# A hybrid decoder layer on one core: full-array recurrence products, paired value products, a new order of the output projection, and new costs in the kernel's planning clock

## The chip, the cores and the metric

One of the eight cores of a Trainium2 chip runs the whole layer in one launch. The metric is device time in microseconds (us), from the first to the last instruction and what little lies around them. TensorE (PE) multiplies, VectorE (DVE), ScalarE (ACT) and GpSimd (POOL) work on vectors, and SyncE (SP) issues the DMAs. The program is static: each engine works through its own list in order, and a step waits by semaphores for steps of other engines.

## The reference

512 tokens of width 2048. A combined projection of the normed input feeds three branches; their gated outputs are concatenated, projected again and added to x.

```python
h = _rms(x, norm_g[l]); proj = h @ w_in[l]
pa, pb, pc = _split(proj, (A_COLS, B_COLS, C_COLS))
ya = _rwkv7(...) * silu(ga)            # 12 heads of 64; recurrence below
yb = _pool(pu, ...) * silu(pg)         # trailing means, 4 groups
yc = _stick_breaking(qc, kc, vc, ...) * silu(gc)   # 12 heads of 64, strictly causal
x = x + concatenate([ya, yb, yc]) @ w_out[l]

def step(state, inp):                  # per token, 64x64 state per head
    sa = einsum('bhvk,bhk->bhv', state, -kk_t)
    state = state * w_t + sa x (kk_t * a_t) + v_t x k_t
    return state, einsum('bhvk,bhk->bhv', state, r_t)
```

## The kernel before

**Projections.** The input projection has 57 column tiles of 128. Each tile is the sum over 16 slices of D of three products (`three`: high by high, high by low, low by high part), that is 48 matmuls of 128x128 by 128x512 into a PSUM tile `pj`; the first three tiles (`first`) are made while the inputs arrive, so 54 tiles or 2592 matmuls are `pj`. The output projection has 4 column groups `nb`; each is 192 such matmuls (tile `oacc`), 768 in all, which go over 8 pairs of slices of the branch outputs (`i2`). Before group 0 uses a slice, `split_y` splits it into `yh` (ACT) and `yl` (DVE). Every 128x1024 piece of weights is fetched by SP (`raw`) and split by ACT (`wh`) and DVE (`wl`).

**Branch steps.** The heads go in six pairs. The generators `rwkv(p)`, `attention(p)` and `pooling(g)` issue the branch work between the projection's matmuls: after each of them `pump()` lets every generator go on whose time has come. That time comes from `Pace`, a clock that the kernel keeps while it is built: it adds an assumed cost to `now` for each matmul and to a due time for each result, and `need(..., margin=)` says from when a step may be issued. `pump(True)` issues whatever is next without asking for the time. A list scheduler behind the kernel orders each engine's list, guided by program order and its own costs.

**One pair of the recurrence.** `rwkv(p)` makes decays and keys (`dec`, `av`, `ss`: products of 512 columns), then `bk` and `amr`, whose products `gm` give the triangular blocks `lt` and `rx`. The blocks of `lt` go to DRAM (`s1`), come back as `nblk` and `xblk`, are inverted in 30 steps on DVE (`pr`, `xblk`), go back through `s2` into `lt` and are completed by two groups of 32x32 products (`q1`, `q2`). Then 8 chunks of 64 tokens follow one another, each a chain: product `w`, copy to `wsb`, product `u`, copies into `uv`, product `s`, new state `uv` of the next chunk. The output `y` has two more products. Each of the five products is one of 64 columns per head, in its half of the array's rows or columns. At the end come norm sums (`bn`, `mu`, `var`) and the gate. Pair p+1 starts its `amr` when pair p's chunks are issued. Attention has score products `z` (the low part over half the rows), scans on DVE, transposes `wT`, and value products `o` per head.

**The end.** Before the output projection the kernel drains all generators by `pump(True)`; the pooling products wait for the last pair. The order of the slices is a0 to a5, c0 to c5, b0 to b3.

Of the kernel before, what the change touches and what calls it, by code (L numbers as in the profile page):

```python
# [8 lines left out]
F32 = mybir.dt.float32  # L9
# [43 lines left out]
BANKS = {"pj": 2, "g": 3, "c": 3}  # L53
# [150 lines left out]
def hybrid_trunk_kernel(ctx: ExitStack, tc: tile.TileContext, x, xT, w_in, w_out, vecs, consts, up_w, pool_w, out, tap=None):  # L204
# [15 lines left out]
    tp = ctx.enter_context(tc.tile_pool(name="tp", bufs=14))  # L220
# [57 lines left out]

    hh = [hp.tile([P, T], F32R, tag=f"hh{k}", name=f"hh{k}") for k in range(KT)]
# [14 lines left out]
    for pl, tag, parts in ((ap, "q2", 1), (ap, "k2", 1), (ap, "w3", 1), (rp, "bk", 2), (rp, "bkt", 2), (rp, "rx", 2),  # L294
                           (rp, "uv", 2), (rp, "amr", 3), (ap, "wt", 2)):
        xt = pl.tile([P, parts, T], F32, tag=tag, name=name("x"))
# [209 lines left out]
    def rwkv(p):  # L506
# [13 lines left out]
        mm(dec, upl[lo, 0:P], wd2[lo, :], False, True)  # L520
# [4 lines left out]
        mm(av, upl[hi, P:2 * P], ad2[hi, :], False, True)  # L525
# [35 lines left out]
        amr = rp.tile([P, NC_, 3, C], F32, tag="amr", name=name("amr"))  # L561
        for h, s in ((0, lo), (1, hi)):
# [7 lines left out]
        dve.tensor_tensor(amr[:, :, 2, :], r3, e[:, :, 1:], ALU.mult)  # L570
# [7 lines left out]
        lt = rp.tile([P, NC_, C], F32, tag="lt", name=name("lt"))  # L578
        ms = strict.rearrange("p (o t) -> p o t", o=1)
        mi = incl.rearrange("p (o t) -> p o t", o=1)  # L580
        for half in range(2):
            cs = slice(4 * half, 4 * half + 4)
            for h, s, other in quad:
                yield need(*([amr, bk] if half == 0 and h == 0 else []), tag="g")
# [6 lines left out]
                dve.tensor_tensor(lt[s, cs, :], g4[s, :, 0, :], ms[s].to_broadcast([HD, 4, C]), ALU.mult)  # L591
# [6 lines left out]
        for h in range(2):  # L598
            for b in range(2):
                r0 = h * HD + b * B  # L600
                dma(out=s1v[:, :, h, b, :], in_=lt[r0:r0 + B, :, b * B:(b + 1) * B])
# [30 lines left out]
        for h in range(2):  # L632
            for b in range(2):
                r0 = h * HD + b * B
                dma(out=lt[r0:r0 + B, :, b * B:(b + 1) * B], in_=s2v[:, :, h, b, :])
# [416 lines left out]
```

## Time and profile before

| | |
|---|---|
| median of 3 runs | 1089.75 us (1088.41 to 1089.97) |
| the profiled execution | 1089.68 us, span 1088.0 us |
| PE busy | 1066.2 us (98%) |
| DVE, ACT, POOL busy | 737.6 (68%), 427.8 (39%), 143.1 us (13%) |

The profile counts PE as busy while a matmul is anywhere in its pipeline, so a share of 98% says that it seldom stood empty, not that it worked at its peak. What a step costs is read from the start of the last matmul before it to the start of one behind it.

### The profile page before, as it was taken

To read this page: it belongs to the slowest core of one execution; us is meant where nothing else is said; L and a number is where in the kernel's file an instruction comes from. 1 tells how busy PE (TensorE), PEld (TensorE's weight loads), DVE (VectorE), ACT (ScalarE), POOL (GpSimd) and SP (SyncE) were. 2 spreads that over 40 slices of the span, in tenths; PEclk is the share of its full clock that TensorE was granted. 3 is DMA by queue.
4 is the path that set the end of the run, shared out by engine and by line. 5 is a ranking of instruction groups with operands and counts; after the bars stand their busy time and mean duration, and the time that the engine had idled before them with its cause. 6 is when DMAs were issued, how large, how long until landed. Compare 5 with 4: busy or idle time off the path is not lost.

```text
span 1088.0 us, 14731 instructions
## 1 busy us (share of the span) xinstructions
PE 1066.2 (98%) x5552; PEld 801.3 (74%) x5552; DVE 737.6 (68%) x1596; ACT 427.8 (39%) x670; POOL 143.1 (13%) x208
## 2 busy tenths in 40 slices
PE   9998999999999999999999999999999999999998
PEld 7877766687666877668766787667776677888887
DVE  6266978759787797778877799777986457223232
ACT  6453525235353354334543345524443235111111
POOL 0031113101132011210211102210021111000000
PEclk9999999999999999899999999999999999999999
DMA  9513231132211321113221132112221125444232
GB/s 329 204 63 105 80 93 40 56 92 84 84 48 51 107 85 66 58 59 97 86 76 39 64 115 77 61 58 84 100 78 55 48 94 163 149 154 137 96 137 75
DMA packets 58185, 101.92 MB, mean 94 GB/s; under 512 B 29312, under 2 KB 30720, under 8 KB 58112
## 3 DMA queue, kind: packets, MB, share of 16 engines
q1 hardware_dynamic: 58112, 100.96, 28.2%
q8 instruction: 44, 0.72, 0.3%
q14 instruction: 29, 0.24, 0.1%
HBM read 95.17 MB, written 5.77 MB: 93 GB/s over the span
## 4 chain that ended last, share of the span: by engine, by line
PE 80%; DVE 10%; issue 4%; ACT 2%; DMA 2%; POOL 2%; SPq 0%; POOLq 0%; DVEq 0%; ACTq 0%
PE pj L350 45%; PE oacc L350 15%; PE first L350 3%; PE o L350 2%; PE z L350 2%; DVE w L198 2%; DVE wl L198 2%; PE gm L350 2%; PE y L350 2%; PE w L350 2%; PE wT L354 1%; DVE xblk L198 1%; PE u L350 1%; POOL e L198 1%; PE s L350 1%
## 5 line engine op out<-in xcount | busy, mean ns | idle before, releaser
L350 PE MATMUL pj<-hl,wh 128*128 128x512 f32 x864 | 349.0, 404 | 0.0
L350 PE MATMUL pj<-hh,wh 128*128 128x512 f32 x864 | 347.9, 403 | 1.0 <-DVE u L198 0.8
L350 PE MATMUL pj<-hh,wl 128*128 128x512 f32 x864 | 347.6, 402 | 0.0
L198 DVE TENSOR_TENSOR wl<-raw,wh 128x1024 fp32r<-128x1024 f32 x140 | 172.1, 1229 | 168.6 <-ACT wh L198 162.8
L198 ACT CAST wh<-raw 128x1024 fp32r<-128x1024 f32 x140 | 147.0, 1050 | 312.7 <-PE pj L350 187.5
L350 PEld LDWEIGHTS pj<-hh,wh 128*128 128x128 f32 x864 | 163.1, 189 | 38.0 <-issue 4.4
L350 PEld LDWEIGHTS pj<-hh,wl 128*128 128x128 f32 x864 | 163.2, 189 | 35.4 <-issue 0.4
L350 PEld LDWEIGHTS pj<-hl,wh 128*128 128x128 f32 x864 | 163.1, 189 | 35.5 <-issue 1.2
L350 PE MATMUL oacc<-wl,yh 128*128 128x512 f32 x256 | 100.1, 391 | 0.8 <-DVE wl L198 0.8
L350 PE MATMUL oacc<-wh,yl 128*128 128x512 f32 x256 | 99.6, 389 | 0.0
L350 PE MATMUL oacc<-wh,yh 128*128 128x512 f32 x256 | 99.6, 389 | 0.0
L198 POOL TENSOR_SCALAR e<-e 128x512 f32<-128x512 f32 x28 | 49.0, 1749 | 327.9 <-ACT e L198 327.6
L198 POOL TENSOR_TENSOR d<-u 128x512 f32<-128x512 f32 x25 | 34.2, 1370 | 230.9 <-DVE u L198 148.6
L350 PEld LDWEIGHTS oacc<-wl,yh 128*128 128x128 f32 x256 | 48.0, 188 | 11.5 <-DVE wl L198 1.3
L350 PEld LDWEIGHTS oacc<-wh,yl 128*128 128x128 f32 x256 | 48.1, 188 | 10.0 <-issue 0.2
L350 PEld LDWEIGHTS oacc<-wh,yh 128*128 128x128 f32 x256 | 48.0, 188 | 10.0
L198 DVE TENSOR_TENSOR xblk<-xblk,pr 128x60 f32<-128x60 f32 (+8 forms) x180 | 44.5, 247 | 4.1
L198 ACT ACTIVATE e<-e 128x512 f32<-128x512 f32 x50 | 31.4, 629 | 39.1 <-POOL e L198 38.8
L198 DVE TENSOR_TENSOR_SCAN w<-kon,n 128x512 f32<-128x512 f32 (+3 forms) x48 | 39.3, 841 | 6.6 <-POOL n L198 6.5
L198 DVE TENSOR_TENSOR pr<-xblk,nblk 128x60 f32<-128x60 f32 (+8 forms) x180 | 38.7, 215 | 4.4
L198 DVE TENSOR_TENSOR u<-pj,rstd 128x512 f32<-128x512 f32 x50 | 34.3, 686 | 8.3 <-PE pj L350 7.9
L198 ACT ACTIVATE n<-n 128x512 f32<-128x512 f32 (+1 forms) x72 | 38.9, 557 | 1.3
(195 smaller groups left out, 1262.7 us busy)
## 6 DMA issues: line engine op xcount, KB each, us to landing
raw<-in_w_in SPq DMA_DIRECT2D x108, 512.0 KB, 3.4
raw<-in_w_out SPq DMA_DIRECT2D x32, 512.0 KB, 3.4
xs<-in_x SPq DMA_DIRECT2D x8, 512.0 KB, 4.7
xr<-in_x SPq DMA_DIRECT2D x16, 256.0 KB, 5.3
out<-xr SPq DMA_DIRECT2D x16, 256.0 KB, 3.2
fr<-in_w_in SPq DMA_DIRECT2D x12, 256.0 KB, 7.4
nblk<-s SPq DMA_DIRECT2D x24, 128.0 KB, 4.9
x<-in_xT SPq DMA_DIRECT2D x5, 512.0 KB, 7.4
```

The costliest lines, as they stand in the source:

```text
L198: return call(*args, **kw)
L350: pe.matmul(o, lhsT, rhs, start=start, stop=stop)
L354: pe.transpose(o, src, ident)
```

## The change

1. The recurrence works with the full array. `amr` gets four 64-column parts, zero outside the head's rows, and stays in one place; `lt` gets a zeroed half for each head. Each of the products w, u, s and y then covers both heads in one matmul (128 columns, u 64). They share one PSUM tile `wus` per chunk; `y` gathers four chunks in a bank of its own. The copies into `wsb` become two, and the products `se` move from DVE to POOL. `gm`, and the low parts of `dec`, `av` and `z`, use all 128 rows (`kl2` is filled by POOL).
2. The value products of both heads stand next to each other, in halves of the columns.
3. The slices of the output projection go in the order `Y_ORDER`, with a5 and c5 last, and nothing is drained before it: `split_y` drains by `pump(True)` what its slice needs. Pooling no longer waits for the last pair.
4. `Pace` assumes other costs: more for DVE and POOL operations and for fp32 matmuls.

```diff
@@ -50,7 +50,7 @@
-BANKS = {"pj": 2, "g": 3, "c": 3}
+BANKS = {"pj": 2, "g": 3, "c": 2, "y": 1}
...
+Y_ORDER = [0, 1, 2, 3, 4, 10, 11, 12, 13, 14, 6, 7, 8, 9, 5, 15]
...
-                return 0.05 + n * 0.0011
-            return 0.08 + n * (0.0028 if f == "tensor_scalar" else 0.0033)
-        if f in ("tensor_scalar", "tensor_copy", "memset") and not any(self.key(a) in self.read_psum for a in ins):
+                return 0.2 + n * 0.0015
+            return 0.1 + n * 0.0031
+        if f == "tensor_tensor_scan":
+            n *= 2
+        if f in ("tensor_scalar", "memset"):
             n *= 0.5
-        return 0.065 + n * 0.00104
+        return 0.165 + n * 0.00104
...
-            c = max(n / 2400.0, m * 0.00083)
+            c = max(n / 2400.0 + 0.010, 0.19 * m / 128)
-            c = max(4 * max(n, 64) / 2400.0, 0.1) * (0.6 if m <= 64 or rhs.shape[0] <= 64 else 1.0)
+            c = max(4 * max(n, 64) / 2400.0, 0.214 if m > 64 else 0.1) * (0.6 if m <= 64 or rhs.shape[0] <= 64 else 1.0)
...
-        mm(av, upl[hi, P:2 * P], ad2[hi, :], False, True)
+        mm(av, upl[:, P:2 * P], ad2, False, True)
...
-        amr = rp.tile([P, NC_, 3, C], F32, tag="amr", name=name("amr"))
-        for h, s in ((0, lo), (1, hi)):
+        for h, s, other in quad:
+            pool.memset(amr[other, :, h, :], 0.0)
-        dve.tensor_tensor(amr[:, :, 2, :], r3, e[:, :, 1:], ALU.mult)
+        dve.tensor_tensor(amr[lo, :, 2, :], r3[lo], e[lo, :, 1:], ALU.mult)
+        pool.tensor_tensor(amr[hi, :, 3, :], r3[hi], e[hi, :, 1:], ALU.mult)
...
-                    rhs = amr[s, cc, 0:3:2, :] if h == 0 else amr[s, cc, 1:3, :]
-                    mm(g[:, j * P:(j + 1) * P], bk[s, cc, :, :], rhs)
+                    mm(g[:, j * P:(j + 1) * P], bk[:, cc, :, :], amr[:, cc, h:4:2, :])
...
-        xt = tmp("xt")
-        dve.transpose(xt, lt.rearrange("p c t -> p (c t)"))
-        xt3 = xt.rearrange("p (c t) -> p c t", t=C)
+        xt = tmp("xt", NC_ * B)
+        xt3 = xt.rearrange("p (c t) -> p c t", t=B)
+        for h in range(2):
+            dve.transpose(xt3[h * HD:h * HD + B], lt[h * HD:h * HD + B, :, h, 0:B])
...
-            yield need(amr, uv, tag="c", margin=TIGHT)
-            wps = cb("w")
-            for h, s, o in quad:
-                mm(wps[s, 0:C], amr[:, cc, h, :], uv[:, cc, h, :])
+            yield need(amr_flat, uv, tag="c", margin=TIGHT)
+            wus = cb("wus")
+            wps, ups, sps = wus[:, 0:P], wus[:, P:P + C], wus[:, 2 * P:3 * P]
+            mm(wps, amr[:, cc, 0:2, :], uv[:, cc, :, :])
             wsb = rp.tile([P, C], F32, tag="wsb", bufs=2, name=name("wsb"))
-            dve.tensor_copy(out=wsb, in_=wps[:, 0:C])
+            dve.tensor_copy(out=wsb[lo, :], in_=wps[lo, 0:C])
+            dve.tensor_copy(out=wsb[hi, :], in_=wps[hi, C:P])
             if not last:
                 se = rp.tile([P, C], F32, tag="se", bufs=2, name=name("se"))
                 for h, s, o in quad:
-                    dve.tensor_scalar(se[s, :], uv[s, cc, h, :], ec[s, cc:cc + 1], None, ALU.mult)
-            yield need(wsb, lt, tag="c", margin=TIGHT)
-            yps = cb("y")
-            for h, s, o in quad:
-                mm(yps[s, 0:C], uv[s, cc, h, :], amr[s, cc, 2, :], True, False)
-            ups = cb("u")
-            for h, s, o in quad:
-                mm(ups[s, 0:C], lt[s, cc, :], wsb[s, :])
-            for h, s, o in quad:
-                dve.tensor_copy(out=uv[s, cc, h, :], in_=ups[s, 0:C])
-            yield need(uv, tag=None if last else "c", margin=TIGHT + 0.1)
+                    pool.tensor_scalar(se[s, :], uv[s, cc, h, :], ec[s, cc:cc + 1], None, ALU.mult)
+            yield need(wsb, lt, tag="y" if cc % 4 == 0 else None, margin=TIGHT)
+            mm(ups, lt[:, cc, :, :], wsb)
+            if cc % 4 == 0:
+                ybank = bank("y", "y")
+            yps = ybank[:, (cc % 4) * P:(cc % 4 + 1) * P]
+            mm(yps, uv[:, cc, :, :], amr[:, cc, 2:4, :], True, False)
+            dve.tensor_copy(out=uv[lo, cc, 0, :], in_=ups[lo, :])
+            dve.tensor_copy(out=uv[hi, cc, 1, :], in_=ups[hi, :])
+            yield need(uv, margin=TIGHT + 0.1)
             if not last:
-                sps = cb("s")
+                mm(sps, bkt[:, cc, :], uv[:, cc, :, :])
                 for h, s, o in quad:
-                    mm(sps[s, 0:C], bkt[:, cc, h * HD:(h + 1) * HD], uv[:, cc, h, :])
+                    dve.scalar_tensor_tensor(uv[s, cc + 1, h, :], sps[s, h * C:(h + 1) * C], ec[s, cc:cc + 1], se[s, :], ALU.mult, ALU.add)
+            mm(yps, uv[:, cc, :, :], rx[:, cc, :, :], False, True)
+            if cc % 4 == 3:
+                y4 = ybank.rearrange("p (c h t) -> p c h t", c=4, h=2)
+                yo = y[:, (cc - 3) * C:(cc + 1) * C].rearrange("p (c t) -> p c t", t=C)
                 for h, s, o in quad:
-                    dve.scalar_tensor_tensor(uv[s, cc + 1, h, :], sps[s, 0:C], ec[s, cc:cc + 1], se[s, :], ALU.mult, ALU.add)
-            for h, s, o in quad:
-                mm(yps[s, 0:C], uv[:, cc, h, :], rx[:, cc, h, :], False, True)
-            act.copy(out=y[:, cc * C:(cc + 1) * C], in_=yps[:, 0:C])
+                    act.copy(out=yo[s], in_=y4[s, :, h, :])
...
+            kl2 = ap.tile([P, T], F32R, tag="kl2", name=name("kl2"))
+            pool.tensor_copy(out=kl2[s, :], in_=klo[s, :])
+            pool.tensor_copy(out=kl2[other, :], in_=klo[s, :])
-                    mm(z[:, off:off + (i + 1) * P], q2[s, i * P:(i + 1) * P], klo[s, 0:(i + 1) * P], False, True)
+                    mm(z[:, off:off + (i + 1) * P], q2[:, i * P:(i + 1) * P], kl2[:, 0:(i + 1) * P], False, True)
...
+        o = None
+        for js, width in (((0,), 512), ((1, 3), 512), ((2,), 256)):
+            parts = []
+            for h in range(2):
+                yield need(*head[h].values(), tag="g", margin=MARGIN + 2.0)
+                home = {(0, 0): "q2", (0, 1): "k2", (1, 0): "kl2", (2, 0): "q2", (2, 1): "k2"}.get((js[0], h))
+                wt = ap.tile([P, T], F32, tag=home, name=name("wt"))[:, 0:width] if home else tmp("wt", width)
+                (dve.tensor_copy if h == 0 else act.copy)(out=wt, in_=tps[:, 0:width])
+                parts.append(wt)
+            yield need(*parts, vt, tag="g" if o is None else None)
+            if o is None:
+                o = gb("o")
+            for j in js:
+                for h, s in ((0, lo), (1, hi)):
+                    mm(o[s, j * P:T], vt[:, j, s], parts[h][:, pos[j]], j == 0, j == 2)
+        while ("cg", p) not in got:
+            yield None
+        y = yt[Y_TILE[("c", p)]]
+        dve.tensor_tensor(y, o, y, ALU.mult)
...
-        while ("pg", g) not in got or not done.get(("gn", NPAIR - 1)) or not done.get(("att", NPAIR - 1)):
+        while ("pg", g) not in got:
...
-    first = [cb("first") for _ in range(NFIRST)]
+    first = [bank(("c", "c", "y")[n], "first") for n in range(NFIRST)]
+    for h, s, other in quad:
+        pool.memset(amr[other, :, 2 + h, :], 0.0)
+        pool.memset(lt[s, :, 1 - h, :], 0.0)
-    while len(tasks) > 1:
-        pump(True)
+    ready = {n: ({"a": "gn", "b": "pool", "c": "att"}[br], i) for (br, i), n in Y_TILE.items()}
-        k = order[i]
-        while 6 <= k < 10 and tasks:
+        k = Y_ORDER[i]
+        while not done.get(ready[k]):
-    tags = ("c",) * 3 + ("g",) * 3 + ("pj",) * 2
+    tags = ("pj", "pj", "g", "g", "g", "c", "c", "y")
-                    k = order[i]
+                    k = Y_ORDER[i]
```

The static order shows where this puts the recurrence. PE, before, a chunk of the last pair (`uv_1264`) while `pj` tiles 1287 and 1318 are projected:

```order
L350 MATMUL w_1311_7593<-uv_1264_7311,amr_1166_6710 64x64
L350 MATMUL y_1314_7604<-amr_1166_6710,uv_1264_7311 64x64
L350 MATMUL pj_1287_7455<-hh15_109,wl_1290_7459 128x512
L350 MATMUL pj_1318_7627<-hh0_94,wh_1308_7564 128x512
L350 MATMUL u_1315_7607<-wsb_1312_7596,lt_1170_6722 64x64 x2
L350 MATMUL pj_1318_7627<-hl0_110,wh_1308_7564 128x512
L350 MATMUL pj_1318_7627<-hh0_94,wl_1309_7565 128x512
L350 MATMUL pj_1318_7627<-hh1_95,wh_1308_7564 128x512
L350 MATMUL pj_1318_7627<-hl1_111,wh_1308_7564 128x512
L350 MATMUL s_1316_7616<-uv_1264_7311,bkt_1168_6720 64x64
```

PE, after, a chunk of pair 4 (`uv_1210`), which now stands behind the last `pj` and behind the first 48 `oacc`:

```order
L363 MATMUL wus_1224_7447<-uv_1210_7332,amr_94 128x128
L363 MATMUL y_1223_7439<-amr_94,uv_1210_7332 128x128
L363 MATMUL wus_1224_7447<-wsb_1225_7449,lt_95 128x64
L363 MATMUL wus_1224_7447<-uv_1210_7332,bkt_1113_6709 128x128
L363 MATMUL y_1223_7439<-rx_1114_6710,uv_1210_7332 128x128
L363 MATMUL wus_1227_7463<-uv_1210_7332,amr_94 128x128
```

The products of a chunk now follow each other directly; the same holds for all 8 chunks of pair 4 and 7 of pair 5, where projection matmuls stood between them.

PE, before, the second group of 32x32 products of the last pair (`q2_1275`), with `pj` on both sides:

```order
L350 MATMUL pj_1251_7265<-hl13_123,wh_1253_7268 128x512
L350 MATMUL pj_1251_7265<-hh13_107,wl_1254_7269 128x512
L350 MATMUL pj_1251_7265<-hh14_108,wh_1253_7268 128x512
L350 MATMUL pj_1251_7265<-hl14_124,wh_1253_7268 128x512
L350 MATMUL q2_1275_7393<-lt_1170_6722,w1_1273_7360 32x32 x16
L350 MATMUL w_1277_7415<-uv_1264_7311,amr_1166_6710 64x64 x2
L350 MATMUL pj_1251_7265<-hh14_108,wl_1254_7269 128x512
L350 MATMUL pj_1251_7265<-hh15_109,wh_1253_7268 128x512
```

PE, after, the last pair (`lt_95` is the one `lt` now) from the end of the seventh slice pair of the output projection's group 0 (`oacc_1203`):

```order
L363 MATMUL oacc_1203_7290<-wh_1334_8113,yl9_8146 128x512
L363 MATMUL bn_1283_7779<-sh_1281_7775,bone_r_86 128x512
L363 MATMUL bn_1283_7779<-sl_1282_7776,bone_r_86 128x512
L367 MATMUL vt_1286_7785<-kon_83,d_927_5670 128x128 x4
L363 MATMUL wus_1292_7839<-uv_1285_7784,amr_94 128x128
L363 MATMUL y_1295_7848<-amr_94,uv_1285_7784 128x128
L363 MATMUL q1_1288_7797<-xt_1287_7794,lt_95 32x32 x16
L363 MATMUL q2_1290_7817<-lt_95,w1_1289_7798 32x32 x16
L363 MATMUL wus_1292_7839<-wsb_1293_7841,lt_95 128x64
L363 MATMUL wus_1292_7839<-uv_1285_7784,bkt_1268_7646 128x128
L363 MATMUL y_1295_7848<-rx_1269_7647,uv_1285_7784 128x128
L363 MATMUL wus_1296_7856<-uv_1285_7784,amr_94 128x128
```

All of the last pair's way from `lt`'s solve to its chunks now lies between two stretches of the output projection. Between its last `gm` and `q1` stand 52 `oacc`; 28 `oacc` of group 1 stand among its last products, and the rest, 572, behind.

## Rows read from the trace of the kernel before

**Rows 1.** Two stretches (us): length, busy time (instructions) by engine, PEclk, DMA share, GB/s
```profile
42.00:908.00 866.00, 851.19 (x4619) 624.40 (x4617) 660.95 (x1502) 366.11 (x594) 137.06 (x199) 0.99 0.24 76
908.00:1088.00 180.00, 175.41 (x771) 144.26 (x769) 54.89 (x58) 35.10 (x36) 5.43 (x2) 1.00 0.39 132
```

**Rows 2.** Tile pj on PE: ns min/median/max, first and last start, forms
```profile
L350 PE MATMUL pj<-hh,wh x864: 387/389/799, 42.1 to 907.3; 128*128 128x512 f32 x173
```

**Rows 3.** Timeline of PE, full-array step: start, length, what, count
```profile
227.43 0.39 PE L350 MATMUL pj<-hh,wl 128*128 128x512 f32 x1
227.66 0.60 PE L354 MATMUL tr<-kon,bk 128*128 128x128 f32 x4
...
228.33 0.39 PE L350 MATMUL pj<-hl,wh 128*128 128x512 f32 x1
```

**Rows 4.** Timeline of PE, a step of the recurrence
```profile
181.97 0.40 PE L350 MATMUL pj<-hh,wh 128*128 128x512 f32 x1
182.30 0.34 PE L350 MATMUL s<-uv,bkt 128*64 128x64 f32 x4
...
183.02 0.39 PE L350 MATMUL pj<-hh,wl 128*128 128x512 f32 x1
```

**Rows 5.** A group of PE: busy us, mean ns of one, idle before
```profile
L350 PE MATMUL s<-uv,bkt 128*64 128x64 f32 x168 | 16.2, 248 | 0.2 <-DVE uv L198 0.2
```

**Rows 6.** Timeline of PE, the score products of one head
```profile
394.26 0.40 PE L350 MATMUL pj<-hl,wh 128*128 128x512 f32 x1
...
397.46 0.40 PE L350 MATMUL pj<-hh,wh 128*128 128x512 f32 x1
```

**Rows 7.** Timeline of PE, the value products of one head
```profile
420.83 2.37 PE L350 MATMUL o<-wt,vt 128*64 128x512 f32 x8
```

**Rows 8.** Timeline of PE and DVE, the links of a chunk (two places)
```profile
461.55 0.33 PE L350 MATMUL u<-wsb,lt 64*64 64x64 f32 x4
...
461.93 0.48 DVE L198 COPY uv<-u 64x64 f32<-64x64 f32 x2 [0.24 <-PE u L350]
...
860.34 0.34 PE L350 MATMUL s<-uv,bkt 128*64 128x64 f32 x4
...
860.75 0.60 DVE L198 SCALAR_TENSOR_TENSOR uv<-s,ec,se 64x64 f32<-64x64 f32 x2 [0.70 <-PE s L350]
...
861.38 0.35 PE L350 MATMUL w<-uv,amr 128*64 128x64 f32 x4
...
861.79 0.23 DVE L198 COPY wsb<-w 128x64 f32<-128x64 f32 x1 [0.44 <-PE w L350]
```

**Rows 9.** Timeline of SP's queue around one block solve: start, length of issuing, what
```profile
490.10 3.25 SPq L212 DMA_DIRECT2D s<-lt  x4
...
497.54 1.81 SPq L212 DMA_DIRECT2D nblk<-s  x4
...
531.76 0.55 SPq L212 DMA_DIRECT2D s<-xblk  x1
...
537.87 0.92 SPq L212 DMA_DIRECT2D lt<-s  x2
```

**Rows 10.** The page: groups (busy us, mean ns) and DMA issues (us to landing)
```profile
L198 POOL TENSOR_SCALAR e<-e 128x512 f32<-128x512 f32 x28 | 49.0, 1749 | 327.9 <-ACT e L198 327.6
...
L198 DVE TENSOR_TENSOR xblk<-xblk,pr 128x60 f32<-128x60 f32 (+8 forms) x180 | 44.5, 247 | 4.1
...
L198 DVE TENSOR_TENSOR pr<-xblk,nblk 128x60 f32<-128x60 f32 (+8 forms) x180 | 38.7, 215 | 4.4
L198 DVE TENSOR_TENSOR u<-pj,rstd 128x512 f32<-128x512 f32 x50 | 34.3, 686 | 8.3 <-PE pj L350 7.9
...
nblk<-s SPq DMA_DIRECT2D x24, 128.0 KB, 4.9
```

**Rows 11.** One more stretch, columns as in the first group
```profile
444.00:447.00 3.00, 3.00 (x11) 1.84 (x11) 1.21 (x5) 1.10 (x2) 0.00 (x0) 0.50 0.00 0
```

**Rows 12.** Who PE waited for: us in total, times, longest
```profile
PE w L350 <- DVE uv L198: 4.2, 5, 1.2
```

More of the change, by code (lines that the diff above doesn't have):

```diff
@@ L276, in load_constants @@
         dve.tensor_scalar(nvec[:, 12:13], vec[:, V_QN:V_QN + 1], HD ** -0.5, None, ALU.mult)
+    amr_flat = rp.tile([P, NC_ * 4 * C], F32, tag="amr", name="amr")
+    amr = amr_flat.rearrange("p (c a t) -> p c a t", c=NC_, a=4)
+    lt = rp.tile([P, NC_, 2, C], F32, tag="lt", name="lt")
     hh = [hp.tile([P, T], F32R, tag=f"hh{k}", name=f"hh{k}") for k in range(KT)]
@@ L293, in hybrid_trunk_kernel @@
     KQ = 4
-    for pl, tag, parts in ((ap, "q2", 1), (ap, "k2", 1), (ap, "w3", 1), (rp, "bk", 2), (rp, "bkt", 2), (rp, "rx", 2),
-                           (rp, "uv", 2), (rp, "amr", 3), (ap, "wt", 2)):
-        xt = pl.tile([P, parts, T], F32, tag=tag, name=name("x"))
+    for pl, tag, parts in ((ap, "q2", 1), (ap, "k2", 1), (ap, "w30", 1), (rp, "bk", 2), (rp, "bkt", 2), (rp, "rx", 2),
+                           (rp, "uv", 2), (None, "amr", 3), (ap, "w20", 1), (ap, "w21", 1)):
+        if pl is None:
+            xt = amr_flat[:, 0:parts * T].rearrange("p (k t) -> p k t", k=parts)
+        else:
+            xt = pl.tile([P, parts, T], F32, tag=tag, name=name("x"))
         k = len(xk)
@@ L519, in rwkv @@
         mm(dec, uph[:, 0:P], wd2, True, False)
-        mm(dec, upl[lo, 0:P], wd2[lo, :], False, True)
+        mm(dec, upl[:, 0:P], wd2, False, True)
         lam = sigmoid(dec, bias=nvec[:, p:p + 1], post=neg_half)
@@ L583, in rwkv @@
             for h, s, other in quad:
-                yield need(*([amr, bk] if half == 0 and h == 0 else []), tag="g")
+                yield need(*([amr_flat, bk] if half == 0 and h == 0 else []), tag="g")
                 g = gb("gm")
@@ L600, in rwkv @@
                 r0 = h * HD + b * B
-                dma(out=s1v[:, :, h, b, :], in_=lt[r0:r0 + B, :, b * B:(b + 1) * B])
+                dma(out=s1v[:, :, h, b, :], in_=lt[r0:r0 + B, :, h, b * B:(b + 1) * B])
         for half in range(2):
@@ L634, in rwkv @@
                 r0 = h * HD + b * B
-                dma(out=lt[r0:r0 + B, :, b * B:(b + 1) * B], in_=s2v[:, :, h, b, :])
+                dma(out=lt[r0:r0 + B, :, h, b * B:(b + 1) * B], in_=s2v[:, :, h, b, :])
         while ("v", p) not in got:
@@ L676, in rwkv @@
                 r0 = h * HD
-                mm(q2[r0:r0 + B, cc * B:(cc + 1) * B], w1[r0 + B:r0 + C, cc * B:(cc + 1) * B], lt[r0 + B:r0 + C, cc, B:C])
+                mm(q2[r0:r0 + B, cc * B:(cc + 1) * B], w1[r0 + B:r0 + C, cc * B:(cc + 1) * B], lt[r0 + B:r0 + C, cc, h, B:C])
         for h in range(2):
             r0 = h * HD
-            dve.tensor_copy(out=lt[r0:r0 + B, :, B:C], in_=q2[r0:r0 + B, :NC_ * B].rearrange("p (c t) -> p c t", t=B))
+            dve.tensor_copy(out=lt[r0:r0 + B, :, h, B:C], in_=q2[r0:r0 + B, :NC_ * B].rearrange("p (c t) -> p c t", t=B))
         done[("mid", p)] = True
@@ L771, in attention @@
             act.copy(out=k2[other, :], in_=k[s, :])
+            kl2 = ap.tile([P, T], F32R, tag="kl2", name=name("kl2"))
+            pool.tensor_copy(out=kl2[s, :], in_=klo[s, :])
+            pool.tensor_copy(out=kl2[other, :], in_=klo[s, :])
             blocks = {}
             for segs, width in ((((3, 0),), 512), (((2, 0), (0, 384)), 512), (((1, 0),), 256)):
-                yield need(q2, k2, klo, tag="g")
+                yield need(q2, k2, kl2, tag="g")
                 z = gb("z")
@@ L812, in attention @@
                 act.copy(out=vt, in_=vps.rearrange("p (j c) -> p j c", j=4))
-            wt = ap.tile([P, 1280], F32, tag="wt", name=name("wt"))
-            pos = {}
-            off = 0
-            for js, width in (((0,), 512), ((1, 3), 512), ((2,), 256)):
-                yield need(*blocks.values(), tag="g", margin=MARGIN + 2.0)
+        o = None
[3 more added lines that the diff above has]
+                yield need(*head[h].values(), tag="g", margin=MARGIN + 2.0)
                 tps = gb("wT")
-                o2 = 0
+                pos = {}
+                off = 0
                 for j in js:
-                    pos[j] = off + o2
+                    pos[j] = slice(off, off + T - j * P)
                     for i in range(j, 4):
-                        transpose(tps[:, o2:o2 + P], blocks[(i, j)])
-                        o2 += P
-                dst = wt[:, off:off + width]
-                (dve.tensor_copy if js[0] != 1 else act.copy)(out=dst, in_=tps[:, 0:width])
-                off += width
-            yield need(wt, vt, tag="g")
-            o = gb("o")
-            for j in range(4):
-                mm(o[s, j * P:T], vt[:, j, s], wt[:, pos[j]:pos[j] + T - j * P], j == 0, j == 3)
-            while ("cg", p) not in got:
-                yield None
-            y = yt[Y_TILE[("c", p)]]
-            dve.tensor_tensor(y[s, :], o[s, :], y[s, :], ALU.mult)
+                        transpose(tps[:, off:off + P], head[h][(i, j)])
+                        off += P
+                home = {(0, 0): "q2", (0, 1): "k2", (1, 0): "kl2", (2, 0): "q2", (2, 1): "k2"}.get((js[0], h))
[12 more added lines that the diff above has]
+        dve.tensor_tensor(y, o, y, ALU.mult)
         done[("att", p)] = True
@@ L993, in _pack @@
     w_in = w_in.reshape(len(TILES), P, KT * P)
-    order = list(range(6)) + list(range(10, 16)) + list(range(6, 10))
-    wo = f["w_out"][0].reshape(KT, P, 4, 512)[order]
+    wo = f["w_out"][0].reshape(KT, P, 4, 512)[Y_ORDER]
     w_out = np.ascontiguousarray(wo.reshape(KT // 2, 2, P, 4, 512).transpose(3, 0, 2, 1, 4)).reshape(4, KT // 2, P, 1024)
```

14 lines of the change are left out of this document (6 added, 8 removed).

## The prediction

> **What bounds the kernel now.** I read the two stretches first. The projections run from 42 to 908 us, and PE is busy in 851 of these 866 us; the output projection follows from 908 on without a break [rows 1, 2]. DVE is busy in 661 us of the first stretch, 76%, so it has room. PE sets the end in both stretches. In the second one 771 matmuls take 175.4 busy us, 0.228 each; in the first, too, the next product starts 0.23 after a `pj` [rows 1, 3]. I take 0.227. The 2592 `pj` then need 588 us of the 866. The other 278 us are branch steps, what they cost on entering and leaving, and waits: this is what the change works on.
>
> Next I read what one step costs, from the last `pj` before it to the second `pj` behind it, less two times 0.227. Four full-array transposes: 228.33 - 227.43 - 0.454 = 0.446 [rows 3], that is 4 x 0.109 and almost nothing for entering. A step of the recurrence, s and y of both heads, eight records of 64 columns in half-array shapes: 183.02 - 181.97 - 0.454 = 0.596 [rows 4]. Its records overlap: 168 of s, 0.248 long on the mean, fill only 16.2 us, and the four here 0.34 [rows 4, 5]. Eight records of 64 columns at 0.053 each, two at a time, stream some 0.21; the rest, nearly 0.4, is lost before the first and behind the last record. The score products, eight records of which four use half the rows, cost 397.46 - 394.26 - 0.454 = 2.75, for 2560 columns that at the rate of `pj` would take 1.14 [rows 6].
>
> **The change, part by part.**
>
> *Full-array products.* I count every branch step of the changed kernel at the full-array price, 0.109 for a record of up to 128 columns, two records to a fp32 matmul, 0.23 for one of 512 columns, and 0.016 for entering:
> - w and s: 90 matmuls x 0.218 = 19.6; y: 96 x 0.218 = 20.9; gm: 96 x 0.218 = 20.9;
> - u, 48 of 64 columns: between 0.11 (columns) and 0.218 (as if 128): 0.16 taken, 7.7 (5.1 to 10.5);
> - z: 12 heads x 8 records; the two short ones of each kind are not shown at full size, so between their columns and 0.19 each: 16.8 (14 to 19);
> - 216 transposes x 0.109 = 23.5; 96 sums of 512 columns (dec, av, ss, qm, bn, mu, var) x 0.23 = 22.1;
> - q1 and q2, unchanged in half-array shapes, about 0.9 each: 10.8; four pooling products and one small one 4.3; some 240 entries 3.8;
> - o: now both heads side by side, see below, 19.3.
>
> The sum is 170 us, where before stands 278 with its waits. The recurrence gives the most: a chunk cost some 1.8 (0.6 for s and y, about as much for each of the two other steps), now 4 x 0.218 + 0.16 + 3 x 0.016 = 1.08; the score products give about (2.75 - 1.4) x 12 = 16.
>
> A rule of the Trainium skill speaks against this part: the page TensorEngine Tiling (Array Packing), section Theoretical Speedup, says that with contraction or output of at most 64 the tiled array gains up to twofold because tiles run side by side. The trace agrees that they do, by the overlap of s [rows 5]. By that rule alone each of 186 products w, s and y would stream 0.107 longer and nothing would come back, 20 us lost; by the rows the 0.4 around each step is worth more.
>
> *Paired value products.* One head's eight records take 2.37 [rows 7], so a pair of heads 4.74 without entering. If the halves of the columns overlap as the records of s do, both heads take (512 + 384 + 128 + 256) x 4 / 2.4 GHz = 2.13, in three groups of which each pays about 0.36 for the change of shape: 3.2 per pair, 19.3 in all. If they don't overlap it is 5.3 per pair, 12.8 us more in all.
>
> *Other edits.* Two copies into `wsb` for one (+10 us on DVE), `se` off DVE (-22), `kl2`, `se` and memsets on POOL: all are off PE's path as long as DVE stays near its 76% and POOL, busy in 137 of 866 us, comes in time; the price if POOL doesn't is a rival below. The due times are longer, so steps have more room: the order has at least 0.9 us of PE work between any two links of a chunk in the projections. I leave the waits there as they were, some 13 us (the largest is 4.2, the next 3.1, twelve more down to 0.2) [rows 12], and add 4 for the clock and small losses as before.
>
> *What moves.* By the order, the two last pairs don't get done beside the projections. Pair 4's bn, vt, q1, q2, chunks, mu and var, and all of pair 5 from dec on stand in the output projection: 31 of the 170 us. So the projections end at 42 + 588 + 139 + 13 + 4 = **786 us** instead of 908.
>
> *What the moved steps cost there.* Their chain has no projection matmul between its links; PE waits. A chunk by [rows 8]: s to DVE 0.41, two state updates 0.60, to w 0.03; w to DVE 0.41, two copies 0.47 (0.23 each), to u 0.05; u to DVE 0.38, two copies 0.48, to s 0.05: 2.9 us, of which PE works 1.08.
> - Pair 4: q1 and q2 with their copies about 3.4, seven and a half chunks 21.5, then the norm: thirteen ACT and DVE operations of 512 columns, taken at DVE's 0.69 [rows 10], two sums and the hand-overs, about 11. That is 36; PE works in 12 of it (with dec and av of pair 5): 24 us bare.
> - Pair 5, dec to gm: two sigmoids, scans and six 512-wide DVE operations, some 18 us, of which pair 4's last norm steps and 43 `oacc` cover 15: 3 bare.
> - Pair 5, last gm to q1: eviction and issue 0.5; until the last nblk is issued 499.35 - 493.35 = 6.0; its landing 4.9; the solve 83.2 / 6 = 13.9 and 4.7 of other DVE work that the order puts into it; from the s2 issue to the last lt issue 538.79 - 531.76 = 7.0, and about 2 for that to land; transposes 0.8 [rows 9, 10]. Sum 39.8. Beside it PE has 52 `oacc` (11.8) and 2.3 of steps: 25 bare.
> - Pair 5, q1 to its gate: as for pair 4, less the 28 `oacc` (6.4): about 36 - 6.4 - 9 = 21 bare.
>
> Together **73 us** of bare waiting. In the long ones PE's clock will not stay up: in 444 to 447 us, after a stretch in which PE waited more than a microsecond, the granted clock was 0.50, 1.2 instead of 2.4 GHz, and 11 matmuls filled 3 us [rows 11]. At that level the three products of a chunk add about 0.6 to it, 9 us for sixteen chunks, the sums 3, and the `oacc` behind each long wait some 2 to 3: **17 us**, with bounds 0 and 22.
>
> *Sum.* 786 + 768 x 0.229 = 176 for the output products, + 31 + 73 + 17, + 4 for the last sum and its store as before, is a span of 1087; the waits in the projections and the clock are taken at the upper half of what they may be (with longer due times 10 instead of 13, and 15 instead of 17 since the first chunks still run at the high level): 1082 to 1087. The profiled execution was 1.7 above its span, and 0.07 below the median shown. I say **1085**: 122 us won in the projections, 118 given back behind them.
>
> **The rivals.**
> - *The bare chain is dearer (slower).* One mechanism: a chunk in the output projection takes longer than its links, because `se` now comes from POOL and the copy into `uv` waits for it. POOL needs 1.75 us for 512 columns [rows 10], so about 0.4 for 64, and two of them still fit into the 1.3 us from the state update to that copy. At 3.7 us a chunk it adds 0.8 x 16 = 13: 1098. It decides from 0.3 us a chunk on. The same comes if the solve's DMAs are later than in [rows 9].
> - *The bare chain is cheaper (faster).* The clock stays up, or POOL and DVE, idle otherwise, answer sooner, and the waits of the projections shrink to a third: 1085 - 15 - 5 = 1065.
> - *The small tiles were as good (the change doesn't do what it says).* If full-array fp32 steps paid the same 0.4 around them, the 278 would stay and grow by 20, while the 73 + 17 come on top: about 1195. Against it stand [rows 3], which are such steps.
>
> **How the numbers follow.** Runs of this kernel tell about 0.2% (2.2 us) from no change. The forecast, both sums as worked out with an error of some 12 us, gets 0.54 and reaches from 1073 to 1098; of it 0.26 lies below 1087.5, 0.12 within 0.2%, 0.16 above. The dearer chain gets 0.21 (1098 to 1115), the cheaper one 0.23 (1055 to 1073), the small tiles 0.02. That is faster 0.49, same 0.12, slower 0.39. Leaving out one in ten on each side gives 1064 to 1108. The bounds of u, z and o (6, 5 and 13 us) lie in it.
>
> **What would show it.** The first `oacc` near 786 us; s and y in the projections at about 0.45 for 0.6 and eight z records at 1.4 for 2.75; chunks of some 3 us behind the projections, with DVE ending PE's waits and the granted clock at 0.5; one wait of about 25 us of PE before q1 of pair 5, ended by DVE's `xt`. I am wrong if the projections end after 800, if PE's waits behind them are far from 73 us, or if the value products of two heads don't overlap.

## The result and the profile after

The changed kernel takes **1136.66 us** (median of 4 runs, 1134.22 to 1138.49), the kernel before 1089.86 on the same chip: a ratio of 1.042 (95% interval 1.039 to 1.046), slower. 1085 was predicted, 1064 to 1108 as the range.

The two stretches, as in [rows 1], with the two longest parts of the second one in which the clock is low:

```profile
core 0: us, PE busy (x) PEld busy (x) DVE busy (x) ACT busy (x) POOL busy (x), PEclk, DMA share, GB/s
41.00:822.00 781.00, 745.77 (x3799) 599.34 (x3798) 584.23 (x1233) 345.01 (x540) 210.90 (x288) 0.99 0.25 82
822.00:1129.00 307.00, 248.27 (x1120) 195.84 (x1118) 125.00 (x285) 54.81 (x72) 23.00 (x37) 0.82 0.24 80
843.00:887.00 44.00, 29.83 (x85) 20.72 (x85) 16.63 (x53) 7.93 (x16) 8.25 (x17) 0.50 0.04 15
925.00:986.00 61.00, 29.36 (x150) 22.43 (x151) 27.76 (x118) 0.73 (x2) 5.31 (x12) 0.50 0.16 48
```

The projections end at 822 us instead of 908, but 786 was predicted: 36 us of the miss. The output projection and what is mixed into it take 307 us, where 176 + 31 + 73 + 17 = 297 was predicted: 10 more; PE is idle in 59 of them, and 73 of bare waiting was predicted. The other 6 of the 52 us are the 4 that the forecast took off its own sum and a profiled execution 2 us faster than the median. The steps became as cheap as predicted. The score products of one head, beside [rows 6], and a step of the recurrence, beside [rows 4]:

```profile
133.13 0.39 PE L363 MATMUL z<-k,q 128*128 128x512 f32 x1
...
134.28 0.28 PE L363 MATMUL z<-kl,q 128*128 128x256 f32 x1
134.40 0.39 PE L363 MATMUL pj<-hl,wh 128*128 128x512 f32 x1
...
203.19 0.39 PE L363 MATMUL pj<-hh,wh 128*128 128x512 f32 x1
203.41 0.38 PE L363 MATMUL wus<-uv,bkt 128*128 128x128 f32 x2
203.63 0.39 PE L363 MATMUL y<-rx,uv 128*128 128x128 f32 x2
203.78 0.48 PE L363 MATMUL pj<-hl,wh 128*128 128x512 f32 x1
204.09 0.40 PE L363 MATMUL pj<-hh,wl 128*128 128x512 f32 x1
```

Eight z take 134.40 - 133.13 = 1.27 (before 2.75, predicted 1.4); s and y cost 204.09 - 203.19 - 0.454 = 0.45 (before 0.60). What PE waits for in the projections, beside [rows 12]:

```profile
PE wus L363 <- DVE uv L203: 8.1, 7, 3.2
PE gm L363 <- issue: 5.1, 1, 5.1
PE wus L363 <- DVE wsb L203: 4.6, 5, 2.2
PE vps L367 <- DVE w L203: 4.2, 2, 3.6
PE pj L363 <- DVE wl L203: 4.1, 4, 2.3
```

PE is idle for 35 of 781 us, before for 15 of 866. One chunk behind the projections, beside [rows 8] (the rows of `y` and of the weight loads are left out):

```profile
849.51 0.76 PE L363 MATMUL wus<-uv,amr 128*128 128x128 f32 x2 [0.36 <-DVE uv L203]
850.31 0.46 DVE L203 COPY wsb<-wus 64x64 f32<-64x64 f32 x2 [0.95 <-PE wus L363]
850.83 0.69 PE L363 MATMUL wus<-wsb,lt 128*128 128x64 f32 x2
851.62 0.47 DVE L203 COPY uv<-wus 64x64 f32<-64x64 f32 x2 [0.85 <-PE wus L363]
852.15 0.80 PE L363 MATMUL wus<-uv,bkt 128*128 128x128 f32 x2 [0.64 <-DVE uv L203]
852.99 0.60 DVE L203 SCALAR_TENSOR_TENSOR uv<-wus,ec,se 64x64 f32<-64x64 f32 x2 [0.89 <-PE wus L363]
853.43 0.44 POOL L203 TENSOR_SCALAR se<-uv,ec 64x64 f32<-64x64 f32 x1 [3.32 <-DVE uv L203]
853.73 0.55 PE L363 MATMUL wus<-uv,amr 128*128 128x128 f32 x1 [0.36 <-DVE uv L203]
```

From w to w: 853.73 - 849.51 = 4.22 us. VectorE's parts are as predicted (0.46, 0.47, 0.60). But from the start of a product to its reader it takes 0.80, 0.79 and 0.84 instead of 0.41, 0.38 and 0.41. `se` lies beside the chain. The longest wait behind the projections is the one before the last pair's q1, 19.0 us:

```profile
949.64 0.28 PE L363 MATMUL q<-xt,lt 32*32 32x32 f32 x2 [18.95 <-DVE xt L203]
```

The value products of both heads, one of three groups, beside [rows 7]:

```profile
401.40 1.08 PE L363 MATMUL o<-wt,vt 128*64 128x384 f32 x8
402.42 0.50 PE L363 MATMUL pj<-hh,wh 128*128 128x512 f32 x1
```

These eight records, four of 384 and four of 128 columns, take 1.02 us; one after another, at the 0.109 of [rows 3] for 128 columns, they would take 1.74.

Below, **late** is what remains of the length of the projections when two things are taken off: 2592 x 0.227 = 588 for `pj`, and the steps, each at the shortest spacing of its kind in the changed kernel (a record of 128 columns 0.112, eight z 1.27, and so on). For the changed kernel that is 781.4 - 588.4 - 131 = **62 us**: the 35 idle, and what does not show as idle, such as shorter waits and matmuls at the low clock. The granted clock is 0.50 in three short stretches of these projections, 13 us in all, which cost at most half of that. With all steps in the projections the steps come to 161.

### The profile page after: what moved, and what is told of

The parts are those of the page before. It is cut to its first block, busy times and chain, and to the rows that moved or that the text cites. A ratio compares the mean times of both kernels' runs of the same rounds, so it can differ in the third digit from the quotient of the medians.

```text
span 1132.5 us, 13988 instructions
## 1 busy us (share of the span) xinstructions
PE 1033.4 (91%) x5084; PEld 827.7 (73%) x5084; DVE 731.2 (65%) x1554; ACT 426.7 (38%) x652; POOL 237.6 (21%) x338
## 4 chain that ended last, share of the span: by engine, by line
PE 59%; DVE 18%; issue 7%; POOL 7%; ACT 6%; DMA 1%; SPq 0%; POOLq 0%; DVEq 0%; ACTq 0%
PE pj L363 30%; PE oacc L363 14%; PE wus L363 4%; DVE wl L203 3%; PE first L363 3%; DVE w L203 3%; POOL e L203 3%; DVE uv L203 2%; PE gm L363 2%; ACT e L203 2%; DVE xblk L203 2%; DVE pr L203 2%; ACT n L203 1%; DVE u L203 1%; PE o L363 1%
## 5 line engine op out<-in xcount | busy, mean ns | idle before, releaser
L363 PE MATMUL pj<-hh,wh 128*128 128x512 f32 x864 | 344.4, 399 | 2.0 <-ACT wh L203 1.9
L363 PE MATMUL pj<-hl,wh 128*128 128x512 f32 x864 | 344.7, 399 | 0.0
L203 DVE TENSOR_TENSOR wl<-raw,wh 128x1024 fp32r<-128x1024 f32 x140 | 175.5, 1254 | 146.7 <-ACT wh L203 136.0
L203 POOL TENSOR_SCALAR se<-uv,ec 64x64 f32<-64x64 f32 x84 | 48.4, 576 | 235.0 <-DVE uv L203 230.7
L203 POOL TENSOR_TENSOR d<-u 128x512 f32<-128x512 f32 x25 | 38.2, 1527 | 120.6 <-DVE u L203 82.4
L203 POOL TENSOR_SCALAR e<-e 128x512 f32<-128x512 f32 x28 | 45.6, 1629 | 73.8 <-ACT e L203 67.8
L203 ACT COPY yc<-y 64x256 f32<-64x256 f32 x24 | 8.8, 365 | 99.4 <-PE y L363 99.2
L203 DVE TENSOR_TENSOR xblk<-xblk,pr 128x60 f32<-128x60 f32 (+8 forms) x180 | 40.6, 226 | 5.0
```

Of the source, the lines that this page charges most:

```text
L203: return call(*args, **kw)
L363: pe.matmul(o, lhsT, rhs, start=start, stop=stop)
```

## The experiments

Ratios are to the kernel before on the same chip, with 95% intervals.

**e1: the clock's old numbers.** Both cost functions of `Pace` as before, everything else as changed.

```diff
-        return 0.165 + n * 0.00104
+        return 0.065 + n * 0.00104
...
-            c = max(n / 2400.0 + 0.010, 0.19 * m / 128)
+            c = max(n / 2400.0, m * 0.00083)
```

> The changed kernel with one part undone: the cost functions of the clock (both the engines' and the matmuls') are those of before. Theory A (the new durations make a pair's chain take 165 us instead of 130, so two pairs fall behind the projections): by its order no step stands behind the projections; 588 of pj + 170 of steps + about 20 of waits end the projections at 820, and 177 of output products and 8 of ends follow: 1000 to 1020 us. Rival B (the steps are shorter now, DVE and POOL can't keep up, and PE's waits of about 50 us in the projections have nothing to do with the clock's numbers): the projections end at 850 or later, 1035 to 1060. Rival C (full-array steps give nothing): 1085 or more.

1087.93 us, ratio 0.996 (0.994 to 0.998). A miss for both A and B, and by its time rival C's figure: no step of the recurrence stands behind the projections, as A says, yet they end at 908. They are 588 + 161 + 118 late. PE idles for 62 us:

```profile
PE q L361 <- DVE w L201: 17.5, 6, 4.1
PE wus L361 <- DVE uv L201: 11.0, 11, 1.3
PE q L361 <- DVE xt L201: 8.9, 2, 7.6
PE gm L361 <- issue: 5.1, 1, 5.1
PE ss L361 <- DVE w L201: 4.3, 5, 1.4
```

and the mean granted clock there is 0.97 instead of 0.99. One of the low stretches and the whole of the projections, columns as above:

```profile
154.30:171.30 17.00, 11.15 (x94) 9.43 (x95) 7.34 (x16) 4.78 (x9) 2.27 (x5) 0.51 0.26 72
40.00:908.00 868.00, 806.30 (x4152) 638.61 (x4151) 645.63 (x1461) 364.88 (x578) 227.90 (x323) 0.97 0.25 76
```

Taking every stretch to be at 0.5 or 1.0, a mean of 0.97 over 868 us is some 50 us at the low level (an estimate), so at most some 25 of the 118 are lost to it. From the first gm of the fourth pair to that of the fifth there are 384 pj before and here; the period is 129.8 us before and 128.1 here, so a pair takes about as long as before. C is wrong all the same: PE's busy time in the projections is 806 us, before it was 851. The steps are cheaper, and nearly all of their gain comes back as idle time and low clock.

**e2: `se` back on VectorE.** This is the mechanism of the predicted rival.

```diff
-                    pool.tensor_scalar(se[s, :], uv[s, cc, h, :], ...)
+                    dve.tensor_scalar(se[s, :], uv[s, cc, h, :], ...)
```

> The changed kernel, with only the two scalings into se back on DVE. Theory of the dearer chain as it was predicted (the copy into uv waits for se on POOL): a chunk behind the projections falls from 4.2 to 3.6 us or less, and the 8 us that PE waits for uv in the projections shrink to under 3: 1115 to 1125. Rival (POOL's se lies beside the chain, and the chunk is long for PE's low clock): the chunk stays at 4.2, time 1132 to 1142.

1133.81 us, 1.038 (1.035 to 1.040), as its rival says; the chunk stays near 4.15, the projections end at 821. In these PE waits 3.5 us for uv instead of 8.1, but 7.4 instead of 4.6 for wsb. POOL's `se`, in the changed kernel

```profile
L203 POOL TENSOR_SCALAR se<-uv,ec 64x64 f32<-64x64 f32 x84 | 48.4, 576 | 235.0 <-DVE uv L203 230.7
```

at 576 ns each, is not what makes the chain long.

**e3 and e5: work in PE's gaps.** Matmuls of the identity, which nobody reads, in the last two pairs: 2 behind w, 3 behind u, 3 behind s, and 70 before the last q1. The lines are e5's; e3 writes to columns of `wus` instead of `fb`.

```diff
+            fill(p, fb, 2)
...
+        fill(p - 1, q1[:, 256:384], 70)
```

> The changed kernel with extra matmuls that nobody reads: 2, 3 and 3 of 128 columns behind the three links of each chunk of the last two pairs, and 70 before q1 of the last pair, so that PE has work in its waits. Theory (the low clock makes a chunk long: a link's product to DVE takes 0.80 us at 1.2 GHz and 0.42 at 2.4): the granted clock stays near 1.0, a chunk falls from 4.2 to 3.1, 16 to 25 us less in all: 1112 to 1121. Rival (links are long whatever the clock): chunks stay at 4.2 or grow by the extra work, 1137 to 1150.

> As e3_filled_gaps, but the extra matmuls of the chunks go to a bank of their own, so that no copy has to wait for them (in e3 the copies out of the products' bank waited 0.76 and 1.04 us instead of 0.46 and 0.53). Theory (low clock): the granted clock stays near 1.0 and a chunk falls from 4.2 to about 3.1: with 16 chunks 1112 to 1122. Rival (the links are long whatever the clock, or the extra work stands in their way): 4.2 or more, 1135 or more.

e3: 1153.62, 1.055 (1.052 to 1.059). Its extra products share the bank of w, u and s, and the copies waited for them (0.87 from w and 1.26 from u to the copy):

```profile
857.42 0.43 PE L363 MATMUL wus<-wsb,lt 128*128 128x64 f32 x2 [0.33 <-DVE wsb L203]
857.69 0.89 PE L368 MATMUL wus<-kon 128*128 128x128 f32 x6
858.68 0.48 DVE L203 COPY uv<-wus 64x64 f32<-64x64 f32 x2 [1.32 <-PE wus L368]
```

So it can't price the clock. e5: 1126.41, 1.031 (1.028 to 1.035); the second stretch falls from 307 to 296 us, its mean clock rises from 0.82 to 0.95. The stretch, and a chunk in it (the extra matmuls, `y` and the weight loads left out):

```profile
822.00:1118.00 296.00, 270.20 (x1518) 227.53 (x1517) 125.21 (x285) 55.23 (x72) 23.02 (x37) 0.95 0.27 83
...
853.45 0.46 PE L363 MATMUL wus<-uv,amr 128*128 128x128 f32 x2
853.95 0.46 DVE L203 COPY wsb<-wus 64x64 f32<-64x64 f32 x2 [0.64 <-PE wus L363]
854.46 0.43 PE L363 MATMUL wus<-wsb,lt 128*128 128x64 f32 x2
855.00 0.47 DVE L203 COPY uv<-wus 64x64 f32<-64x64 f32 x2 [0.60 <-PE wus L363]
855.53 0.49 PE L363 MATMUL wus<-uv,bkt 128*128 128x128 f32 x2
856.06 0.60 DVE L203 SCALAR_TENSOR_TENSOR uv<-wus,ec,se 64x64 f32<-64x64 f32 x2 [0.58 <-PE wus L363]
856.80 0.35 PE L363 MATMUL wus<-uv,amr 128*128 128x128 f32 x1
```

The chunk is 3.35 us, and a product reaches its reader in 0.50 to 0.54, though the extra matmuls run between its records. The low clock makes a chunk about 0.9 us longer, where 0.6 was taken. The chunk stays above the 3.1 expected, and the whole gain is 10 us by the medians, short of the 14 expected at least.

**e4: POOL relieved, old numbers.** `se` and one copy into `kl2` on VectorE, the other on ScalarE.

> The changed kernel with the clock's cost functions of before, and se and the two copies into kl2 taken off POOL (se and one copy on DVE, the other on ACT). If POOL's new work is what makes PE wait in the projections: 10 to 20 us under the run with the old costs alone. If it is not: within 5 us of that run, or above it by what DVE gets (25 us more work in the projections).

1087.70, 0.995 (0.993 to 0.997), within 5 us of e1: POOL's new work does not make PE late there.

**e6, e7, e8: one number of the clock.** The fixed part of a VectorE instruction, 0.165 in the changed kernel, is set to 0.065, 0.100 and 0.130.

```diff
-        return 0.165 + n * 0.00104
+        return 0.100 + n * 0.00104
```

> The changed kernel with one number of the clock as before: the fixed part of a VectorE instruction, 0.065 instead of 0.165 us. By its order nothing of the recurrence stands behind the projections. Theory P (this number decides how far apart a pair's steps are placed; too small, and PE reaches them before VectorE is done; too large, and the last pairs fall behind the projections): PE waits 45 to 60 us in the projections as with all the old costs, 1070 to 1090. Rival (the waits come from the other new numbers or from the order of VectorE's queue, whatever the spacing): waits of 35 us as in the changed kernel without its open stretch, 1025 to 1050.

> The same number at 0.100 us. By its order three chunk steps and the norm of the last pair stand behind the projections, nothing else. Theory P: fewer waits than at 0.065, 30 to 45 us in the projections, and 10 to 15 behind them: 1055 to 1085, the best of the series or near it. Rival: as at 0.065, within 8 us.

> The same number at 0.130 us. By its order one pair stands behind the projections from gm on, where the changed kernel has two. Theory P: about 60 us bare behind the projections and 30 to 40 of waits in them: 1085 to 1110. Rival (what stands behind the projections costs little): 1060 or less.

| fixed part | projections end | PE idle in them | time | ratio |
|---|---|---|---|---|
| 0.065 (e6) | 922 | 60 | 1104.89 | 1.012 (1.009 to 1.015) |
| 0.100 (e7) | 899 | 52 | 1081.46 | 0.988 (0.984 to 0.993) |
| 0.130 (e8) | 865 | 49 | 1124.77 | 1.031 (1.027 to 1.034) |
| 0.165 (changed) | 822 | 35 | 1136.66 | 1.042 (1.039 to 1.046) |

This one number moves the time by 5%, with its best where the pairs just fit beside the projections. Theory P holds in its shape, but its reason only in part. The times at 0.065 and 0.130 lie above what was expected, and at 0.100 and 0.130 PE waits 7 to 9 us more. With a larger number fewer pairs lie in the projections, too: counted per pair whose chunks lie there, PE idles 10 us in e1 and in e6 (six pairs) and 9 in the changed kernel (four). What the wider spacing takes away is the wait before q1 and q2, 26 us in e1 and none in the changed kernel's projections; the waits at the chunks stay. e7 is faster than both kernels (its trace is of an execution of 1085 us).

**e9, e10, e11: links cut.** The chunk products read constants (part of `kon`) instead of `uv` and `wsb`.

```diff
-            mm(ups, lt[:, cc, :, :], wsb)
+            mm(ups, lt[:, cc, :, :], wsbz)
```

> The kernel before, with the chunk products reading constants that are ready instead of uv and wsb: all instructions stay, also VectorE's, but PE never waits for a link of the recurrence (the result is not the reference's). If the 0.4 us lost around each half-array step is the price of its shape, as predicted: 1075 to 1092. If it was waiting for VectorE that the busy time hides: 1060 or less.

> e1_old_costs with the same cut: the chunk products read constants (the result is not the reference's). Theory W (full-array steps are cheap, 163 us by the shortest of each kind, and 116 us of the projections of e1 are waiting, a good part of it at the links of the recurrence, 180 entries at 0.15 to 0.5): 1030 to 1060. Rival (the steps themselves cost it): within 8 us of e1's 1088.

> The changed kernel with the same cut. Theory W: the 26 chunks or so in the projections lose their waits (13 us by the rows of uv and wsb, up to 20 with hidden ones), the 16 chunks behind them fall from 4.2 to 1.5 us, 40 less: 1075 to 1090. Rival (what makes PE late in the projections is the attention and the solve): the projections stay within 8 us of 822 and only the open stretch shrinks: 1090 to 1100.

e9, in the kernel before: 1071.34, 0.980 (0.977 to 0.983), between the two expectations. Waits at the links were worth 20 us there. PE stays busy in 839 of 850 us, so besides 588 for `pj` the steps still take 251; how much of that is waiting that the busy time hides, e9 doesn't tell. e10, with the old numbers: 1082.37, 0.991 (0.988 to 0.995). That misses theory W and lies within the rival's 8 us of e1; it does not prove the rival, for PE still waited:

```profile
PE q L363 <- DVE w L201: 15.9, 5, 4.2
PE wus L363 <- DVE wsb L201: 13.2, 15, 2.0
```

No product reads `wsb` any more. What is left to tie them is the bank: w, u and s of a chunk share one of two, where before each took the next of three; no run gave them back. The rows are of an execution of 1091 us, 9 above the median, with a mean clock of 0.95 in the projections. e11, in the changed kernel: 1091.84, 0.999 (0.997 to 1.002), as its rival says. The second stretch falls from 307 to 263 us, so the links of the 16 chunks behind the projections cost 44:

```profile
829.00:1092.00 263.00, 226.62 (x1120) 184.01 (x1118) 124.74 (x285) 54.85 (x72) 23.82 (x37) 0.90 0.29 93
```

The projections don't fall (788 us long for 781, in an execution 5 us above the median).

**e12: half of the copies on ScalarE**, on e7. One of the two edits; the other is the same for the copy into `uv`.

```diff
-            dve.tensor_copy(out=wsb[hi, :], in_=wps[hi, C:P])
+            act.copy(out=wsb[hi, :], in_=wps[hi, C:P])
```

> e7_dve_fixed_100 with the upper half's copies into wsb and uv on ScalarE, beside VectorE's for the lower half. If the chain's length on VectorE (two copies one behind the other, 0.47 us) and its full queue make PE wait: 5 to 15 us less than e7, 1066 to 1077. If not, or if ScalarE's queue (0.6 us an instruction) holds the copies up: 1078 or more.

1081.70, 0.989 (0.986 to 0.993): no better than e7, as expected if VectorE's two copies are not what makes PE wait.

**e13, e14, e15: VectorE relieved.** The subtraction into `wl` is left out, a quarter of VectorE's work, but the clock still counts it.

```diff
-        dve.tensor_tensor(wl, raw, wh.bitcast(F32), ALU.subtract)
-        return wh, wl
+        pace.record("dve", "tensor_tensor", wl, [raw, wh])
+        return wh, wh
```

> e1_old_costs without the 140 subtractions into wl (1.25 us each, 175 of VectorE's 722 us); the clock still counts them, so the planned order stays, and the products that read wl read wh (the result is not the reference's). In e1 the projections take 867 us: 588 of pj, 161 of steps by the shortest of each kind, 118 late. Theory V (steps come late because VectorE's queue is three quarters full and their operand stands behind others in it): late falls to 40 to 70 us, 1005 to 1050. Rival U (the spacing is too short for the links' own length, whatever stands in the queue): late falls by under 25 us, 1065 to 1085.

> The changed kernel without the subtractions into wl, in the same way. Its projections take 781 us: 588 of pj, 131 of steps, 62 late. Theory V: late falls to 20 to 35, the projections end at 780 to 795, and the open stretch, whose chain has no wl in it, stays within 8 us of 307: 1092 to 1110. Rival U: the projections end at 810 or later, 1120 or more.

> The kernel before without the subtractions into wl, in the same way. In it half-array steps keep PE busy by themselves, and cutting the links of the recurrence gave 20 us. Theory V: little is late, so 1068 to 1090. Rival (its steps too are mostly waiting for VectorE): 1060 or less.

e13: 1073.36, 0.982 (0.980 to 0.984); late falls from 118 to 105, as rival U says. e14: 1113.98, 1.019 (1.018 to 1.021); the projections end at 803 and late falls from 62 to 44, between theory V and U. e15: 1067.36, 0.977 (0.974 to 0.979), 21 us in the projections, just under theory V's range. VectorE's queue accounts for 13 to 21 us in each, whatever the shape of the steps; in the changed kernel 4 of its 18 are the wait of `pj` for `wl` itself. It is not the main cause with the old numbers.

**e16, e17: the links spread**, on e1.

```diff
-TIGHT = 0.05
+TIGHT = 0.3
```

> e1_old_costs with one number changed: the distance that the plan keeps between a chunk's operand and its product, 0.30 us more than reckoned instead of 0.05. By its order nothing falls behind the projections. Theory U (with the old numbers the three links of a chunk are placed about 0.3 us nearer than they are long): of the 29 us that come late at the chunk's products 15 to 25 go, 1062 to 1075. Rival (the pairs' chain is then longer, and the lateness comes back elsewhere): within 6 us of 1088.

> The same with 0.60 us. By its order only the norm's last sums of the last pair stand behind the projections. Theory U: nearly all of the 29 us gone, 1060 to 1075. Rival: 1082 or more.

1080.00, 0.989 (0.986 to 0.992), and 1083.66, 0.994 (0.991 to 0.996). e16 lies between the expectations, e17 at the rival's: late is 112 and 111 instead of 118. PE's idle time before the chunk products stays as it was (14 us in e1, 14 and 15 here). Before q1 and q2 it falls from 26 to 13 in both, and before bn and vps it rises from 1 to 16 and 12: PE meets another operand that is not ready.

## Why the prediction was wrong

*The prices held.* Steps beside the projections cost 131 us at their shortest, predicted 139. The value products of both heads overlap: 15.7 us for six pairs from the first record to the next product, some 18 with entering and leaving, 19.3 predicted. The rival "small tiles as good" said that full-array steps would pay the same 0.4 around them. They don't: s and y cost 0.45 for 0.60, eight z 1.27 for 2.75, and PE's busy time falls by 45 us in e1. Its sum, nothing gained, is what e1's time shows, but for another reason, the lateness. By the Trainium skill, page TensorEngine Tiling (Array Packing), section Theoretical Speedup, the small tiles would have kept up; the s and y of 0.60 and 0.45 us decide against it here.

*The order held.* Pairs 4 and 5 stood behind the projections as read from it, and PE waits there with the clock at 0.50, as foreseen.

*The step that failed* is "I leave the waits there as they were, some 13 us, ... and add 4". Late is 62 us, not 17: 45 more, less 8 for the cheaper steps, is the 37 by which the projections are longer than the 744 us predicted. The reason given, that longer due times leave room, was no measurement: 13 us had been measured in a kernel whose PE lost some 0.4 us at each small step, and VectorE worked on meanwhile. With cheap steps PE reaches the next operand sooner. e1 agrees without any step moved: 161 + 118, as long as before, with 62 us idle for 15. Behind that may stand the sentence on the bound, "PE sets the end in both stretches": PE was busy, but e1's period of 128 us for 130 suggests that the pairs' chain as planned was hardly shorter than PE's work. No run measured that chain alone.

*What the 62 us are* is settled only in part. 18 of them go when VectorE has a quarter less to do (e14), and up to 7 are the low clock. They don't go when `se` leaves POOL (e2), nor when the links of the recurrence are cut (e11). Where one wait was taken away others grew (e2, e16, e17), so no single one can be named for the rest, and the cause stays open. Not tested are the banks: two for w, u and s together, three before.

*The chunk price* is the second step: 2.9 us and 0.6 for the clock, against 4.22. The 0.7 too little, sixteen times, is 11 us, about the miss of 10 in the second stretch; that they agree is partly luck, since the wait before q1 came out 6 shorter. The links were read at the high clock, and the clock was charged for the products' columns alone; the way from a product's start to VectorE takes 0.4 longer at 1.2 GHz (0.80 against 0.41), three times a chunk. e5 gives 0.9 of it back. The wait before the last pair's q1 was 19.0 us, predicted 25, ended by `xt`, as said.

*The rival "dearer chain"* had the sign, and a chunk dearer by 0.7 us, but the wrong mechanism, and its 1098 to 1115 does not reach the result: `se` takes 0.58 us on POOL, more than the 0.4 estimated, and is still ready in time; e2 excludes it.

*Where the change loses.* Its cheap steps would pay, but the clock's new numbers hold the pairs so far apart (155 to 184 us from gm to gm for the first five) that two of six fall behind the projections, where PE has little else to do. With the old numbers all pairs fit, but PE waits for them (e1). With the fixed part at 0.100 the same products are 1.2% faster than before, and with the old numbers and wider links 1.1% (e16).

## What to carry to other kernels

When steps on the busiest engine get cheaper, price the waits anew: the time between two steps was also the time in which the other engine made the next operand. In a plan with due times the numbers are not there to be right one by one; ask of each what it moves out of the cover, and scan it. And read a dependent link at the clock at which it will run, hand-over included.

## What was not expected of the hardware

The low clock lengthens the way from a product to its reader by more than was charged for the product's columns. From the product's start to its reader on VectorE it is 0.79 to 0.84 us at a granted clock of 0.50, which is 0.39 to 0.43 more than in [rows 8], and 0.50 to 0.54 with PE kept at work (e5). The u of the changed kernel shows 0.47 just before its clock falls (1.00 from 838 to 843 us, 0.50 from 843.3 to 847), against 0.79 behind:

```profile
842.79 0.43 PE L363 MATMUL wus<-wsb,lt 128*128 128x64 f32 x2 [1.89 <-DVE lt L203]
843.26 0.46 DVE L203 COPY uv<-wus 64x64 f32<-64x64 f32 x2 [0.53 <-PE wus L363]
```

And extra products into other columns of the same bank held a copy up (e3: 1.26 us from u to the copy, 0.54 in e5 with a bank of their own); whether the chip or the semaphores of this program make it wait, no run tells.
